# Layer 0's feed-forward: three pairs by token halves and eight by seven products in two groups, with six products ahead of the second projection

## The chip, the core and the metric

The kernel runs on one core of one Trainium2 chip. The metric is device time in microseconds (us) of one execution; the comparison is between medians of several executions. The engines are TensorE (PE; its weight loads are PEld), VectorE (DVE), ScalarE (ACT), GpSimd (POOL) and SyncE (SP), which issues most transfers. Every engine works through its own queue in order.

## What is computed

A decoder trunk of two layers on 512 tokens of width 1024, in float32. Cut to what matters here:

```python
def swiglu_ffn(x, w_up, w_down):
    gate, up = jnp.split(x @ w_up, 2, axis=-1)
    return (jax.nn.silu(gate) * up) @ w_down

# layer 0
h = h + conformer_conv(rmsnorm(h, norm_mix[0]), ...)   # pw1, GLU, causal conv of 31 taps, LayerNorm, silu, pw2
h = h + swiglu_ffn(rmsnorm(h, norm_ffn[0]), ffn_w_up[0], ffn_w_down[0])
# then K and V from rmsnorm(h), layer 1: attention and another swiglu_ffn, last rmsnorm
```

The hidden width is 2816. The change lies in layer 0, from the second projection (`pw2`) of the convolution module to the end of the feed-forward.

## The kernel before, in words

**Precision.** Float32 operands are split in a high and a low part (`whi`, `wlo` of a weight chunk; likewise of the activations), and `mm3` (L376) issues three matmuls: high by high, high by low, low by high. For every weight chunk of 512 KB ScalarE makes `whi` (L294) and VectorE `wlo` (L297). The first twelve chunks of the plan (`NATIVE`) aren't split; one plain float32 matmul stands for three.

**The plan of weights.** `chunk_plan` (L90) lists all chunks in the order of use. `advance` (L299) is called at each use: it loads up to nine chunks ahead (six `raw` buffers), splits up to three ahead, and advances `prepare` (L277) by `share` steps.

**Pairs.** The hidden width is cut into eleven pairs of 256 gate and 256 up columns. Layer 0 treats them in two ways (`HALVES0`, L35):

- Pairs 0 to 3 *by token halves*: `ffn_part` (L585) does up products, gates and down products for the first 256 tokens, later again for the last 256. A pair has four up chunks and two down chunks in each half. The second half uses the twin form `mm2` (L407): one matmul of `whi` with high and low part side by side (512 columns) and one of `wlo` (256).
- Pairs 4 to 10 *by seven products*: a Strassen scheme over the two token halves and the two halves of the 1024 inputs. `SevenPair.take` (L821) multiplies a block of weights (A11, A12, A22, or one of the sums S1 to S4) with a block of rows (B11, B12, B21, B22, or one of the sums T1 to T4), 24 matmuls of 256 columns each, and adds the results in PSUM and in a tile `c`. `gates` makes the hidden values, and one down projection over all 512 tokens follows.

The sums S of the weights are made in DRAM: SP copies a block (`copy_sums`, L268), and an accumulating transfer from the GpSimd queue adds the other block (`prepare`, L289). The copies for the first nine units (a unit is one pair of layer 0 or one part of layer 1's weights) are made in two early sets, seven and two. `share` is 0.45 steps per chunk in the halves and 1/4 in the products.

**Order.** The second token half of the convolution (`h1`) runs in the background while TensorE does the first half's `pw2`, up and down: VectorE and the pair ScalarE and GpSimd share the taps (L1010, L1002, L1003). Then come its LayerNorm: `squares`, `sums` (L1059), `scales_a` (L1068 to L1075), `scales_b`, `spread` (L1090), and eight `rows` of z (L1102 to L1104, split at L544 and L545). `job` and `pace` (L327, L337) set this by a list of points (count of chunks used, steps done). TensorE's next work after the first half is three products for first-half tokens, A12 by B21 of pairs 4, 5 and 6 (`FIRST`), whose results are kept in one `quad` buffer; and then `pw2` of the second half, which reads z.

The RMS factors of the feed-forward come from `step1` (L503 to L515: sums over channels on TensorE, `ms` on VectorE, `rs` on GpSimd, a diagonal on ScalarE) and `spread` (L529). In the first half `step1` stands between pair 0 and pair 1, and the spread after half of pair 1, when pair 0 is evacuated (L659, L662, L545).

During the second half, `Rows0.sums` makes T1 to T4 (L1296 on VectorE, then a split each), again by `job`. Then all seven pairs' products run, 46 chunks, followed by the down projection of all seven (14 chunks) and the additions to `h` (L1357), which start the next normalisation.

The program's instructions are put in each engine's queue by a scheduler that goes by a modelled time; `issue_after(x)` keeps an instruction behind `x` on the same engine.

## Time and profile before

| what | value |
|---|---|
| median of three runs | 1046.09 us (1045.9 to 1046.29) |
| the profiled execution | 1048.36 us |
| its span, first to last instruction | 1046.6 us |
| mean granted TensorE clock | 0.997 |
| bytes moved by DMA | 248.33 MB, mean 237 GB/s |
| transfers of sums: accumulates, copies one by one | 88, 52 |

Rows of the timeline read: start, length, engine, line, operation, out<-in, size, count, and in brackets the idle time before and what ended it. Rows of groups read: line, engine, operation, shape, count, then busy time and the mean of one in ns, then idle time before and its causes. Rows of stretches read: from:to, length, busy time of PE, PEld, DVE, ACT and POOL with counts, granted clock, mean share of the 16 DMA engines, GB/s. Lengths of matmuls are modelled and overlap; their pace is in the distance between starts.

The stages around the change in the profiled execution: `pw2` of the first half from 129 us, the first half's up and down from 158 us, the three products from 239 us, `pw2` of the second half from 248 us, the second half's up and down from 271 us, the products of seven from 339 us, their down projection to about 548 us.

### The profile page before, as it was taken

The numbers are of one execution on the slowest core, as the hardware profiler recorded it, in microseconds if no ns is written. First come the engines' busy times: TensorE is split into PE (matmuls) and PEld (weight loads), VectorE is DVE, ScalarE is ACT, GpSimd is POOL, SyncE is SP. The second block draws the span as 40 slices with busy tenths as digits, with TensorE's granted clock in tenths as the row PEclk, the third lists the DMA queues.
The fourth block names the chain that finished last, engine by engine and source line by source line (L and its number), as shares of the span: only waits on it lengthen the run. The fifth ranks groups of instructions, "written<-read, shape, count | busy, mean of one in ns | idle before, by whom it ended". The sixth has DMA issues, their size and how long they took to land.

```text
span 1046.6 us, 17683 instructions
## 1 busy us (share of the span) xinstructions
PE 1032.7 (99%) x6574; PEld 932.7 (89%) x6574; DVE 779.1 (74%) x1206; ACT 612.7 (59%) x1060; POOL 466.6 (45%) x563
## 2 busy tenths in 40 slices
PE   9999998999999999999999999999999999999996
PEld 8888887999988999998888877788989999898995
DVE  3999989978889786773536556678686877868677
ACT  3887896946776565552334555466655555554653
POOL 3999998940444332222214255405442334334131
PEclk9999999999999999999999999999999999999998
DMA  9999846989899988898968776845879888867742
GB/s 351 335 332 195 203 130 173 282 245 272 243 256 253 302 221 283 255 296 251 284 222 240 208 192 183 211 167 150 251 234 312 284 264 266 244 232 222 226 142 80
DMA packets 67282, 248.33 MB, mean 237 GB/s; under 512 B 7579, under 2 KB 13884, under 8 KB 66364
## 3 DMA queue, kind: packets, MB, share of 16 engines
q1 hardware_dynamic: 53804, 199.96, 54.7%
q0 software_dynamic: 12672, 46.14, 24.6%
q8 instruction: 51, 0.84, 0.3%
q10 hardware_dynamic: 720, 1.10, 0.3%
q14 instruction: 35, 0.29, 0.1%
HBM read 241.93 MB, written 97.52 MB: 324 GB/s over the span
## 4 chain that ended last, share of the span: by engine, by line
PE 91%; DVE 4%; ACT 2%; issue 1%; DMA 1%; POOL 1%; SPq 0%; DVEq 0%; ACTq 0%
PE bank L380 20%; PE bank L382 20%; PE bank L381 20%; PE bank L903 9%; PE bank L961 8%; PE bank L412 4%; PE bank L413 2%; PE bank L1442 1%; PE bank L1484 1%; PE bank L1471 1%; DVE bank L1010 1%; ACT pr L1002 1%; PE bank L1059 1%; DVE wlo L297 1%; DMA both<-in_lead_dram 1%
## 5 line engine op out<-in xcount | busy, mean ns | idle before, releaser
L297 DVE TENSOR_TENSOR wlo<-raw,whi 128x1024 fp32r<-128x1024 f32 x246 | 327.1, 1337 | 137.7 <-ACT whi L294 126.9
L294 ACT CAST whi<-raw 128x1024 fp32r<-128x1024 f32 x246 | 257.2, 1049 | 280.9 <-PE bank L381 194.9
L380 PE MATMUL bank<-quad,whi 128*128 128x256 f32 (+1 forms) x976 | 307.2, 317 | 0.0
L381 PE MATMUL bank<-quad,whi 128*128 128x256 f32 (+1 forms) x976 | 306.6, 315 | 0.0
L382 PE MATMUL bank<-quad,wlo 128*128 128x256 f32 (+1 forms) x976 | 305.7, 315 | 0.0
L380 PEld LDWEIGHTS bank<-quad,whi 128*128 128x128 f32 x976 | 185.5, 191 | 12.8 <-issue 1.6
L381 PEld LDWEIGHTS bank<-quad,whi 128*128 128x128 f32 x976 | 186.0, 191 | 11.8 <-issue 0.5
L382 PEld LDWEIGHTS bank<-quad,wlo 128*128 128x128 f32 x976 | 185.6, 191 | 11.8 <-issue 0.4
L854 POOL TENSOR_TENSOR up<-up 128x512 f32<-128x512 f32 x34 | 62.9, 1851 | 283.6 <-ACT up L851 283.6
L1003 POOL TENSOR_TENSOR pr<-pr,pr 128x256 f32<-128x256 f32 x208 | 157.5, 837 | 4.5 <-ACT pr L1002 4.2
L380 PE MATMUL bank<-rows,whi 128*128 128x256 f32 x488 | 138.0, 283 | 0.0
L381 PE MATMUL bank<-rows,whi 128*128 128x256 f32 x488 | 137.8, 282 | 0.0
L382 PE MATMUL bank<-rows,wlo 128*128 128x256 f32 x488 | 137.8, 282 | 0.0
L1010 DVE SCALAR_TENSOR_TENSOR bank<-apad,wdw,bank 128x256 f32<-128x256 f32 x248 | 112.4, 484 | 3.4
L1002 ACT ACTIVATE pr<-apad,wdw 128x256 f32<-128x256 f32 x208 | 98.5, 502 | 15.1 <-POOL pr L1003 13.2
L961 PE MATMUL bank<-quad,w 128*128 128x256 f32 x448 | 98.7, 380 | 0.0
L961 PEld LDWEIGHTS bank<-quad,w 128*128 128x128 f32 x448 | 84.9, 190 | 11.8 <-DVE bank L1010 0.2
L380 PEld LDWEIGHTS bank<-rows,whi 128*128 128x128 f32 x488 | 93.1, 191 | 0.3
L381 PEld LDWEIGHTS bank<-rows,whi 128*128 128x128 f32 x488 | 93.1, 191 | 0.3
L382 PEld LDWEIGHTS bank<-rows,wlo 128*128 128x128 f32 x488 | 93.0, 191 | 0.0
L491 POOL TENSOR_TENSOR tmp<-tmp,tmp 128x256 f32<-128x256 f32 (+1 forms) x28 | 26.8, 956 | 101.9 <-ACT tmp L487 96.7
L412 PE MATMUL bank<-quad,whi 128*128 128x512 f32 x168 | 59.7, 398 | 0.0
(229 smaller groups left out, 1632.9 us busy)
## 6 DMA issues: line engine op xcount, KB each, us to landing
raw<-in_W_dram SPq DMA_DIRECT2D x170, 512.0 KB, 5.7
raw<-sum SPq DMA_DIRECT2D x88, 512.0 KB, 5.5
sum<-in_W_dram SPq DMA_DIRECT2D x52, 512.0 KB, 6.3
sum<-in_W_dram POOLq DMA_DIRECT2D x44, 512.0 KB, 9.5
sum<-sum POOLq DMA_DIRECT2D x44, 512.0 KB, 8.8
sum<-in_W_dram SPq DMA_DIRECT2D x4, 3584.0 KB, 29.7
w<-in_W_dram SPq DMA_DIRECT2D x14, 512.0 KB, 9.7
sum<-in_W_dram SPq DMA_DIRECT2D x4, 1024.0 KB, 29.6
```

Source lines behind the costliest of these rows:

```text
L294: on_act = nc.scalar.copy(hi, src).ins
L297: latest[:] = [on_act, lo_engine[0].tensor_sub(lo, src, f32(hi)).ins]
L380: nc.tensor.matmul(out, w[0], x[0], start=start, stop=False, **kw)
L381: nc.tensor.matmul(out, w[0], x[1], start=False, stop=False, **kw)
L382: nc.tensor.matmul(out, w[1], x[0], start=False, stop=stop, **kw)
L412: nc.tensor.matmul(first[2], first[0], first[1], start=start, stop=False)
L854: pool_op(nc.gpsimd.tensor_mul(gate, gate, c[:, m, :, 1, :]))
L903: nc.tensor.matmul(out, x, w[:, ws], start=first and e == 0 and i == 0, stop=e == 1 and i == 2, skip_group_check=True)
L961: mm = nc.tensor.matmul(self.pb[:, w * W2:(w + 1) * W2], w1_of(ct, w, k), x[k] if x else xg[k][:, tok], start=k == 0, stop=k == KT - 1)
L1002: on_act = nc.scalar.mul(pr, a[:, j:j + W2], tap(j))
L1003: on_pool = pool_op(nc.gpsimd.tensor_add(pr, acc, pr))
L1010: on_dve = nc.vector.scalar_tensor_tensor(yt if i == nd - 1 else c, src, tap(i), c if i else self.shift, op0=ALU.mult, op1=ALU.add)
```

## The change

- Pairs 0 to 2 go by token halves, pairs 3 to 10 by seven products. The eight are cut in two groups of four; each group has its products and then its own down projection with its own additions to `h`. Only the last group starts the next normalisation.
- Six products (A12 of pairs 3 to 8) stand ahead of the second half's `pw2`. Their results lie in one `quad` buffer and two smaller ones in a pool `keep`. `pace` is called before each product and between its halves.
- In the first half, `step1` moves behind the first chunk of pair 1, and pair 0's evacuation behind the third.
- `stamp` holds the last matmul of `mm3`; the small matmuls of `h1`'s LayerNorm in the background are kept behind it.
- The points of `job` change for `h1` and for the sums T; `pace` is called in the loop of products, and the flush of T's job comes after the first group's products.
- `share` is 0.5 in the halves and 0.45 in the products and the first group's down projection, 0.6 in the last one's as before.
- The tiles `c` lie in `quads` for odd pairs and in `z0` for even ones; `z0` has four buffers instead of five. The early copies are now eight units and one.

```diff
-HALVES0 = ((0, 4), (4, 11))
-FIRST = (4, 5, 6)
+HALVES0 = ((0, 3), (3, 11))
+GROUPS0 = ((3, 7), (7, 11))
+FIRST = tuple(range(3, 9))
...
-    plan.extend(("up0", *step) for step in part2_products())
-    downs(*HALVES0[1])
+    for group in GROUPS0:
+        plan.extend(("up0", *step) for step in part2_products(group))
+        downs(*group)
...
+    stamp = [None]
+
     def mm3(out, w, x, start, stop, **kw):
...
-        nc.tensor.matmul(out, w[1], x[0], start=False, stop=stop, **kw)
+        stamp[0] = nc.tensor.matmul(out, w[1], x[0], start=False, stop=stop, **kw).ins
...
-                    if half == 0 and which == 1:
-                        if w == 512 or twin:
-                            rms.step1()
+                    if twin and half == 0 and which == 1 or pending and half + which == 0:
+                        rms.step1()
+                    if half == 1 and which == 0:
                         for p in pending:
                             evac(*p)
                         pending = []
-            if w == 256 and pair == lo and not twin:
-                rms.step1()
+            if pair == lo and not twin:
                 pending.append((pair, full))
...
-    def product(key, block, r, opens, closes=True):
+    def product(key, block, r, opens, between=None):
...
         for which in range(2):
+            if which and between is not None:
+                between()
...
                 for n, (_, f) in enumerate(due):
-                    f()
+                    with tc.issue_after(stamp[0]):
+                        f()
...
-                self.scales_a()
+                with tc.issue_after(stamp[0]):
+                    self.scales_a()
...
-                self.spread()
+                with tc.issue_after(stamp[0]):
+                    self.spread()
...
-        job(second, (base, 0), (base + 8, 19), (base + 13, 22), (base + 26, 40), (base + 30, 45), (base + 34, 50), (base + 35, h1.n_steps - early - 3))
+        job(second, (base, 0), (base + 8, 19), (base + 13, 22), (base + 24, 39), (base + 28, 43), (base + 29, 44), (base + 30, 44),
+            (base + 31, 46), (base + 33, 48), (base + 34, 49), (base + 37, h1.n_steps - early))
...
-        preparing[0], share[0] = prepare(), 0.45
+        preparing[0], share[0] = prepare(), 0.5
...
-    job(rows0.sums(), (base + 11, 0), (base + 19, 8), (base + 26, 14), (base + 32, 17))
+    job(rows0.sums(), (base + 10, 0), (base + 16, 8), (base + 24, 13), (base + 28, 17))
     pw2(h1.z, n1)
     ffn_part(0, 0, x0["ffn0"], HALF[1], n1.rms, twin=True)
-    flush()
...
-    share[0] = 1 / 4
...
+    share[0] = 0.45
+    for group in GROUPS0:
+        lo0, hi0 = group
+        last = hi0 == HALVES0[1][1]
...
+        for pair, a in part2_products(group):
+            if pair not in open_pairs:
+                if pair % 2:
+                    c = quads.tile([P, 2, 2, 2, 256], F32, tag="quad", name=uid("up"))
+                else:
+                    c = z0.tile([P, 2, 2, 2, 256], F32, tag="z0", name=uid("up"), bufs=4)
+                open_pairs[pair] = SevenPair("up0", pair, rows0, c, first.get(pair))
+            pace()
+            open_pairs[pair].take(a)
...
+        flush()
...
             for m in range(4):
                 nc.vector.tensor_add(h[g * 4 + m], banks[m], h[g * 4 + m])
-                nxt.on_h(g * 4 + m)
+                if last:
+                    nxt.on_h(g * 4 + m)
```

71 lines of the change are left out of this document (35 added, 36 removed).

## The prediction

> **What bounds the kernel now.** I read the first part of the page first, then TensorE's waits, then the places where they lie, then the engines by stage.
>
> ```profile
> PE 1032.7 (99%) x6574; PEld 932.7 (89%) x6574; DVE 779.1 (74%) x1206; ACT 612.7 (59%) x1060; POOL 466.6 (45%) x563
> ```
>
> Next the list of TensorE's waits over the whole run (waited for: us in total, times, longest).
>
> ```profile
> PE bank L529 <- ACT tmp L515: 2.1, 1, 2.1
> PE bank L465 <- POOL ones_m L462: 1.0, 1, 1.0
> PE bank L503 <- DVE tmp L491: 1.0, 1, 1.0
> PE bank L949 <- DVE quad L923: 0.5, 2, 0.3
> ```
>
> The reader is to see that TensorE is the bound from end to end: four kinds of wait, 4.6 us of 1046.6. Two of them, 3.18 us together, belong to the first half's RMS statistics (`step1` and the spread). Everything else is decided by how many matmuls are issued and at what pace. The pace is in the starts of neighbouring matmuls, in the timeline of TensorE: 256 columns, then the twin form (512 and 256 columns), then 512 columns in the down projection.
>
> ```profile
> 190.00 0.28 PE L380 MATMUL bank<-quad,whi 128*128 128x256 f32 x1
> 190.12 0.28 PE L381 MATMUL bank<-quad,whi 128*128 128x256 f32 x1
> ...
> 290.12 0.40 PE L412 MATMUL bank<-quad,whi 128*128 128x512 f32 x1
> 290.35 0.28 PE L413 MATMUL bank<-quad,wlo 128*128 128x256 f32 x1
> 290.47 0.39 PE L412 MATMUL bank<-quad,whi 128*128 128x512 f32 x1
> ...
> 500.00 0.39 PE L381 MATMUL bank<-quad,whi 128*128 128x512 f32 x1
> 500.22 0.39 PE L382 MATMUL bank<-quad,wlo 128*128 128x512 f32 x1
> 500.45 0.39 PE L380 MATMUL bank<-quad,whi 128*128 128x512 f32 x1
> ```
>
> So 0.12 us, 0.35 us for a twin pair, and 0.225 us. The busy column (0.28, 0.39) is a modelled length of overlapping instructions and isn't used.
>
> Close behind TensorE comes VectorE, in two stretches (length, PE, PEld, DVE, ACT, POOL busy, clock, DMA share, GB/s).
>
> ```profile
> 145.00:188.00 43.00, 39.83 (x225) 35.89 (x224) 39.88 (x64) 32.72 (x74) 37.85 (x45) 1.00 0.63 187
> 188.00:216.00 28.00, 28.00 (x232) 27.89 (x232) 27.89 (x42) 22.96 (x40) 25.13 (x27) 1.00 0.95 267
> 216.00:240.00 24.00, 24.00 (x191) 23.31 (x191) 15.64 (x25) 10.80 (x15) 8.08 (x9) 1.00 0.88 230
> 302.00:346.00 44.00, 44.00 (x270) 39.15 (x269) 42.64 (x52) 27.47 (x40) 20.05 (x19) 1.00 0.95 262
> ```
>
> VectorE is full while the second half's convolution is finished (to 219 us) and again while the sums T1 to T4 are made (302 to 346 us). Both lie in the stages that the change shortens.
>
> **The change part by part.** (1) *Matmuls.* Pair 3 by halves costs 96 + 48 matmuls of 256 columns in the first half, 144 x 0.12 = 17.3 us, and 32 + 16 twin pairs in the second, 48 x 0.35 = 16.8 us: 34.1 us. By seven products it costs 7 x 24 x 0.12 = 20.2 us, and its down projection 48 x 0.225 = 10.8 us: 31.0 us. Term: **-3.1 us**. Six products ahead instead of three is the same work in another place; splitting in two groups adds none on TensorE.
>
> (2) *`step1` a chunk later.* Now it stands before pair 1 and TensorE waits for the last square sum; the next rows are that wait, the spread's, and what VectorE did between.
>
> ```profile
> 174.05 0.61 PE L503 MATMUL bank<-ones_c,tmp 128*128 128x1 f32 x4 [1.05 <-DVE tmp L491]
> 182.63 0.70 PE L529 MATMUL bank<-tmp,ones_m 128*128 128x256 f32 x2 [2.13 <-ACT tmp L515]
> ...
> 173.92 5.12 DVE L297 TENSOR_TENSOR wlo<-raw,whi 128x1024 fp32r<-128x1024 f32 x3
> 178.96 2.05 DVE L1010 SCALAR_TENSOR_TENSOR bank<-apad,wdw,bank 128x256 f32<-128x256 f32 x4
> 180.92 0.15 DVE L505 TENSOR_SCALAR ms<-bank 128x2 f32<-128x2 f32 x1
> ```
>
> One chunk of 24 matmuls (2.9 us) ahead of `step1` covers its 1.05 us. The spread keeps its distance, two chunks; its lateness comes from the `ms` instruction standing 7 us behind three splits and four taps. In the new order it is reached by TensorE at about 182, a little before 182.6; if a fourth split gets ahead of `ms`, it is 2.8 us late instead. Bounds of the two together: -3.2 to -0.4; I take **-1.7** (the first wait gone, a third of the second).
>
> (3) *The convolution's deadline.* TensorE reaches `pw2(h1)` earlier: 72 matmuls fewer (8.6 us) and what (2) gives. VectorE loses six splits, adds three, and loses one evacuation (L659 and two like it, 2 us). The rows below carry the evacuation's group and the chain's end: last tap, sums, scales, spread, first rows of z.
>
> ```profile
> L659 DVE TENSOR_TENSOR tmp<-bank,rsbc 128x512 f32<-128x512 f32 x4 | 2.6, 679 | 0.0
> ...
> 218.64 0.86 DVE L1010 SCALAR_TENSOR_TENSOR y<-apad,wdw,bank 128x256 f32<-128x256 f32 x2
> ...
> 219.25 2.42 POOL L1014 TENSOR_TENSOR y<-y,pr 128x256 f32<-128x256 f32 x2 [5.31 <-DVE y L1010]
> ...
> 224.34 0.59 PE L1059 MATMUL bank<-y,ones_m 128*128 128x256 f32 x2
> ...
> 229.18 0.95 PE L1068 MATMUL bank<-ident,tmp 128*128 128x1 f32 x8
> ...
> 238.46 1.02 PE L1090 MATMUL bank<-tmp,ones_m 128*128 128x512 f32 x2
> ...
> 245.18 0.75 DVE L545 TENSOR_TENSOR quad<-tmp,quad 128x256 fp32r<-128x256 f32 x2
> ```
>
> From the last tap to z's first two rows it takes 26 us, of which some 8 are waiting for places in TensorE's order. Counting 14 chunks, six products and 4 us of small matmuls from 173.0 us (174.05 less its wait), the new `pw2(h1)` is reached at about 235, so the last tap has to end near 215; VectorE's queue, two splits and an evacuation shorter up to there but with the half's `h` updates in it, ends it between 212 and 217. Six products give 17 us for sums, scales, spread and rows, where 28 us lay between last tap and `pw2(h1)` (238.46, the spread's 0.5 and three products make 247.6). What is queued behind: the first `pw2` chunk waits for z's rows, and all TensorE work behind it. Bounds 0 to +4; I take **+1.0**.
>
> (4) *The second half.* 16.8 us of TensorE go, but only six splits of 1.34 us and an evacuation (four L645 and a split) from VectorE, 10.3 us. From the start of T1 to the products there are 9.5 chunks instead of 12: VectorE brings 2 us more backlog into the products, where it is 73% busy and catches up. `flush` is gone, so T4's split may end inside the first products; T4 is the seventh needed. Bounds 0 to +2.5; I take **+0.5**.
>
> ```profile
> L297 DVE TENSOR_TENSOR wlo<-raw,whi 128x1024 fp32r<-128x1024 f32 x246 | 327.1, 1337 | 137.7 <-ACT whi L294 126.9 <-DMA bias<-fd 4.2 <-DMA raw<-in_W_dram 4.2
> ...
> L645 DVE TENSOR_TENSOR tmp<-bank,tmp 128x256 f32<-128x256 f32 x16 | 6.2, 414 | 1.0 <-ACT tmp L644 0.8
> ...
> L1357 DVE TENSOR_TENSOR h<-bank,h 128x512 f32<-128x512 f32 x8 | 5.5, 686 | 0.1
> ...
> 344.00:472.00 128.00, 128.00 (x1060) 127.33 (x1060) 93.74 (x106) 71.63 (x94) 34.82 (x25) 1.00 0.91 273
> ```
>
> (5) *The sums' transfers.* Pair 3 needs four sums more. `share` 0.45 in the products instead of 0.25 makes 25 x 0.45 = 11 accumulates in each group of 25 products, with a copy to go with most of them in the second group.
>
> ```profile
> q1 hardware_dynamic: 53804, 199.96, 54.7%
> q0 software_dynamic: 12672, 46.14, 24.6%
> ...
> raw<-in_W_dram SPq DMA_DIRECT2D x170, 512.0 KB, 5.7
> ...
> sum<-in_W_dram POOLq DMA_DIRECT2D x44, 512.0 KB, 9.5
> ...
> 350.00:360.00 10.00, 10.00 (x86) 10.00 (x85) 7.73 (x10) 4.30 (x5) 2.14 (x1) 1.00 1.03 333
> ...
> SPq L261 <- DVE wlo L297: 653.0, 221, 13.1
> ```
>
> By the queues' rows a load or copy of 0.524 MB takes the 16 engines 1.50 us (54.7% of 1046.6 for 199.96 MB) and an accumulate 2.93 us (24.6%, 88 of them). A product of 2.88 us then asks for 1.50 + 0.45 x (2.93 + 1.50) = 3.5 us in the second group, 346 GB/s, and some 3.2 in the first: more than the engines have. Cover: loads wait for a free buffer (the 653 us), six buffers of 2.88 us less the landing of 5.7 leave 11 us, and the eight down chunks between the groups (5.4 us each) let the queue catch up. The second group's excess, at the share of 1.03 seen, is 0.5 us x 25 = 12 us, just the cover. Bounds 0 to +6; I take **+0.4**. None of (3) to (5) can gain: TensorE doesn't wait there now.
>
> (6) *At nothing.* Eight more `h` additions on VectorE (0.69 us each) lie beside the second group. The down projection of group 1 needs the last pair's gates only after three chunks (16 us). Buffers: four of `z0`, with odd pairs in `quads`, replace five; at most ten or eleven of eleven `quads` are held. The early copies cover nine units as before, in another division. Were one of these covers gone, it costs an evacuation of one to two microseconds.
>
> Sum: -3.1 - 1.7 + 1.0 + 0.5 + 0.4 = **-2.9 us**. The profiled execution took 1048.36 us (span 1046.6 and 1.8 around it), which makes 1045.5; the median shown is 1046.09, 2.3 lower, and I put the change on that: **1043.2 us**.
>
> **The rivals.** *Everything hides*: the spread's wait goes too and (3) to (5) cost nothing, -3.1 - 3.2 = -6.3, 1039.8. For it: after 10 us TensorE waits nowhere else now. Against: VectorE is full in both stretches.
>
> *VectorE is the clock of the first half*: the last tap ends at 217 or later, z comes 3 to 4 us late, the spread still waits, T's backlog costs 1 or 2. -3.1 - 0.4 + 3.5 + 0.5 = +0.5 at its middle, between -1.5 and +2: 1046.6. The change then shortens the matmuls but not the time. For it: 27.89 of 28 us busy. Against: 216 to 240 has 8 us to spare, and the chain's places were loose.
>
> *The weight loads run dry in the products* (the slower side). [...] If a load lands twice as late as 5.7 us, half of the cover is left; then the first group waits little and the second 6 us: -2.9 - 0.4 + 6.4 = +3.1, 1049.2. It decides from the point where a product's transfers exceed 2.88 us by more than cover over 25, that is 0.25 us with 6 us of cover. For it: 3.5 us asked. Against: the row at 350 moved 333 GB/s with TensorE never waiting. [...]
>
> **How the numbers follow.** Forecast 0.42, everything hides 0.13, VectorE 0.26, loads run dry 0.19. The likeliest gives 1043.2, its own range 1041.5 to 1044.0. From the bounds, 1040.0 to 1049.0 leaves out about 0.1 on each side. About 0.2% (2.1 us) is what a measurement of this kernel can tell from no change: faster 0.55 (the first two), same 0.25, slower 0.20 (the last, and the tail of VectorE's).
>
> **What would show it.** Right: matmul counts of the twin form down by 96, of 512 columns up by 48, the same pace, L503 without a wait, L529's under 2 us; no wait of TensorE before `pw2(h1)` above 1 us, and none on weights in the products. Wrong: a wait on the z rows or on L1059 of several microseconds (3); waits on `wlo` at the first products (4); ACT's cast waiting for `raw` DMAs, landings past 11 us and TensorE waiting on `whi` in the second group (5).

## The result, and the profile after

The changed kernel takes 1055.22 us (median of six, 1053.6 to 1057.82), the kernel before 1045.99 us (six, 1045.65 to 1046.54): ratio 1.0088, 95% interval 1.0077 to 1.0099. It is slower by 9.2 us where 2.9 us less was forecast, and beyond the upper end of the range. The profiled execution took 1054.15 us (span 1052.4 us, mean granted clock 0.996).

Line numbers have moved: the split is now L299 (L297 before), its cast on ScalarE L296 (L294), GpSimd's addition of a tap L1010 (L1003), VectorE's tap L1017 (L1010), `mm3` L384 to L386, the spread of the norm's scale L533, the addition of the block made early to the first product L836 (L831).

First the list of TensorE's waits in the changed kernel (waited for: us in total, times, longest).

```profile
PE bank L386 <- DVE wlo L299: 3.5, 2, 3.0
PE bank L384 <- DVE up L836: 1.7, 1, 1.7
PE bank L533 <- ACT tmp L519: 1.5, 1, 1.5
PE bank L385 <- DVE quad L549: 1.3, 2, 1.1
PE bank L384 <- ACT whi L296: 1.1, 1, 1.1
PE bank L469 <- POOL ones_m L466: 1.1, 1, 1.1
PE bank L956 <- DVE quad L928: 0.2, 1, 0.2
```

Of before's four kinds one is gone (L507, the former L503, no longer waits) and two are smaller (the spread waits 1.5 instead of 2.1 us, L956, the former L949, 0.2 instead of 0.5), but four kinds are new: L386, L385 and two at L384. In time the larger waits lie in two places. The rows of TensorE's timeline, each with the idle time before it and what ended it:

```profile
182.88 0.70 PE L533 MATMUL bank<-tmp,ones_m 128*128 128x256 f32 x2 [1.49 <-ACT tmp L519]
...
196.17 0.39 PE L386 MATMUL bank<-quad,wlo 128*128 128x256 f32 x1 [0.51 <-DVE wlo L299]
...
200.32 0.38 PE L385 MATMUL bank<-quad,whi 128*128 128x256 f32 x1 [1.13 <-DVE quad L549]
...
206.61 0.39 PE L386 MATMUL bank<-quad,wlo 128*128 128x256 f32 x1 [3.04 <-DVE wlo L299]
...
326.05 0.39 PE L384 MATMUL bank<-quad,whi 128*128 128x256 f32 x1 [1.06 <-ACT whi L296]
...
328.27 0.39 PE L384 MATMUL bank<-rows,whi 128*128 128x256 f32 x1 [1.72 <-DVE up L836]
```

6.2 us stand in the first half's up projection, some 40 to 60 us ahead of `pw2(h1)`; 2.8 us at the start of the products. At `pw2(h1)` itself TensorE waits 0.2 us, and none of the listed waits ends with a weight transfer.

What VectorE and GpSimd did during the longest wait, in their timelines (start, length, engine, line, operation):

```profile
199.20 0.48 DVE L1017 SCALAR_TENSOR_TENSOR bank<-apad,wdw,bank 128x256 f32<-128x256 f32 x1
...
200.79 0.47 DVE L1017 SCALAR_TENSOR_TENSOR bank<-apad,wdw,bank 128x256 f32<-128x256 f32 x1
201.18 5.38 DVE L299 TENSOR_TENSOR wlo<-raw,whi 128x1024 fp32r<-128x1024 f32 x1
...
207.47 1.21 DVE L299 TENSOR_TENSOR wlo<-raw,whi 128x1024 fp32r<-128x1024 f32 x1
```

```profile
198.15 2.40 POOL L1010 TENSOR_TENSOR pr<-pr,pr 128x256 f32<-128x256 f32 x2
200.49 0.80 POOL L291 DMA_DIRECT2D sum<-in_W_dram  x1
201.06 4.40 POOL L1010 TENSOR_TENSOR pr<-pr,pr 128x256 f32<-128x256 f32 x6
205.19 1.04 POOL L291 DMA_DIRECT2D sum<-sum  x1
```

A split of the same form takes 1.21 us at 207.47 and 5.38 us at 201.18. GpSimd began six additions 0.12 us before the long one, and they ended at 205.46; 1.21 us before the split's end is 205.35. So the split seems to have done its work after the whole row, and VectorE stood for it. It was not waiting for its cast on ScalarE: the last cast ahead of it ended at 201.46. The taps on VectorE, which have one operand in PSUM (`bank`), take as long when GpSimd adds beside them (0.48 us at 199.20; from 60 to 262 us a mean of 0.485 over 165) as when it is idle (0.482 over 15).

The kernel before has a row of six additions at nearly the same place, and there a split gets in. Its rows of VectorE and GpSimd:

```profile
202.88 1.78 DVE L297 TENSOR_TENSOR wlo<-raw,whi 128x1024 fp32r<-128x1024 f32 x1
```

```profile
200.88 5.78 POOL L1003 TENSOR_TENSOR pr<-pr,pr 128x256 f32<-128x256 f32 x6
```

The split comes in after one addition, and the addition behind it (at 203.54 us in the trace) takes 1.72 us instead of 0.73: here the loss is shared, 0.57 us on the split and 0.99 us on the addition. So the number of additions in a row does not decide alone. What also differs in the traces is how far the records of neighbouring additions overlap: in the long row of the changed kernel each begins about 0.3 us before the one ahead of it ends, in before's row 0.04 us. Over the 18 traces that have these additions (60 to 262 us), 35 splits met two GpSimd instructions (issues of transfers not counted) that overlap by 0.2 us or more, and 33 of them took over 2 us; 97 met instructions that overlap by at most 0.1 us, and 3 did. No run sets this overlap by itself, so it is a sign and not a shown cause.

Two stretches, by engines (length, busy time of PE, PEld, DVE, ACT and POOL with counts, clock, DMA share, GB/s), the first of them shown for before too:

```profile
188.00:216.00 28.00, 23.23 (x172) 22.32 (x171) 27.93 (x33) 17.70 (x31) 21.01 (x25) 0.94 0.89 220
...
208.00:212.00 4.00, 4.00 (x22) 3.90 (x22) 4.00 (x7) 3.85 (x8) 2.68 (x3) 0.65 0.97 249
```

In 188 to 216 us VectorE looks as full as before (27.93 us against 27.89), but with 33 instructions instead of 42: what fills it is standing. And behind the 3.04 us wait the granted clock is down (0.65 over 208 to 212; in the clock's records it is half for 3.41 us, from 207.4). The starts of matmuls show it too:

```profile
207.07 0.28 PE L386 MATMUL bank<-quad,wlo 128*128 128x256 f32 x1
207.19 0.28 PE L384 MATMUL bank<-quad,whi 128*128 128x256 f32 x1
...
207.68 0.42 PE L384 MATMUL bank<-quad,whi 128*128 128x256 f32 x1
207.89 0.42 PE L385 MATMUL bank<-quad,whi 128*128 128x256 f32 x1
```

0.12 us apart at first, 0.21 after. So a wait of 3.0 us cost about 4.5 to 4.7, as an estimate: by the starts, 16 matmuls at 0.21 instead of 0.12 us, 1.5 us come on top, by the granted clock half of the 3.41 us.

### The profile page after: what moved, and what is told of

The parts are those of the page before. It is cut to its first block, busy times and chain, and to the rows that moved or that the text cites. A ratio compares the mean times of both kernels' runs of the same rounds, so it can differ in the third digit from the quotient of the medians.

```text
span 1052.4 us, 17644 instructions
## 1 busy us (share of the span) xinstructions
PE 1032.3 (98%) x6550; PEld 931.5 (89%) x6550; DVE 789.3 (75%) x1212; ACT 610.2 (58%) x1057; POOL 471.3 (45%) x567
## 4 chain that ended last, share of the span: by engine, by line
PE 67%; DVE 1%; ACT 0%; POOL 0%; issue 0%
PE bank L384 18%; PE bank L386 18%; PE bank L385 18%; PE bank L908 9%; PE bank L1462 1%; PE bank L1504 1%; PE bank L1491 1%; PE bank L1620 0%; DVE room L1622 0%; PE bank L1583 0%; DVE room L1631 0%; PE bank L533 0%; PE bank L507 0%; ACT room L1637 0%; POOL rs L1630 0%; DVE room L1635 0%
## 5 line engine op out<-in xcount | busy, mean ns | idle before, releaser
L299 DVE TENSOR_TENSOR wlo<-raw,whi 128x1024 fp32r<-128x1024 f32 x243 | 327.4, 1355 | 126.9 <-ACT whi L296 126.5
L296 ACT CAST whi<-raw 128x1024 fp32r<-128x1024 f32 x243 | 253.8, 1048 | 279.9 <-PE bank L385 197.2
L386 PE MATMUL bank<-quad,wlo 128*128 128x256 f32 (+1 forms) x976 | 307.5, 318 | 3.6 <-DVE wlo L299 3.5
L385 PE MATMUL bank<-quad,whi 128*128 128x256 f32 (+1 forms) x976 | 309.0, 318 | 1.3 <-DVE quad L549 1.3
L384 PE MATMUL bank<-quad,whi 128*128 128x256 f32 (+1 forms) x976 | 308.5, 320 | 1.1 <-ACT whi L296 1.1
L859 POOL TENSOR_TENSOR up<-up 128x512 f32<-128x512 f32 x36 | 67.5, 1875 | 327.3 <-ACT up L856 327.3
L386 PEld LDWEIGHTS bank<-quad,wlo 128*128 128x128 f32 x976 | 186.0, 191 | 16.7 <-DVE wlo L299 4.2
L385 PEld LDWEIGHTS bank<-quad,whi 128*128 128x128 f32 x976 | 186.4, 191 | 14.3 <-DVE quad L549 1.9
L384 PEld LDWEIGHTS bank<-quad,whi 128*128 128x128 f32 x976 | 185.8, 191 | 14.8 <-issue 1.3
L1010 POOL TENSOR_TENSOR pr<-pr,pr 128x256 f32<-128x256 f32 x208 | 153.6, 790 | 6.8 <-ACT pr L1009 6.7
L384 PE MATMUL bank<-rows,whi 128*128 128x256 f32 x512 | 144.9, 283 | 1.7 <-DVE up L836 1.7
L385 PE MATMUL bank<-rows,whi 128*128 128x256 f32 x512 | 144.6, 282 | 0.0
L386 PE MATMUL bank<-rows,wlo 128*128 128x256 f32 x512 | 144.6, 282 | 0.0
L1017 DVE SCALAR_TENSOR_TENSOR bank<-apad,wdw,bank 128x256 f32<-128x256 f32 x248 | 112.5, 485 | 3.5
L384 PEld LDWEIGHTS bank<-rows,whi 128*128 128x128 f32 x512 | 97.6, 191 | 2.2 <-DVE up L836 1.9
L385 PEld LDWEIGHTS bank<-rows,whi 128*128 128x128 f32 x512 | 97.6, 191 | 0.3
L386 PEld LDWEIGHTS bank<-rows,wlo 128*128 128x128 f32 x512 | 97.6, 191 | 0.0
L908 PE MATMUL bank<-wlo,fhi 128*128 128x512 f32 x140 | 55.2, 394 | 0.0
```

The costliest lines, as they stand in the source:

```text
L296: on_act = nc.scalar.copy(hi, src).ins
L299: latest[:] = [on_act, lo_engine[0].tensor_sub(lo, src, f32(hi)).ins]
L384: nc.tensor.matmul(out, w[0], x[0], start=start, stop=False, **kw)
L385: nc.tensor.matmul(out, w[0], x[1], start=False, stop=False, **kw)
L386: stamp[0] = nc.tensor.matmul(out, w[1], x[0], start=False, stop=stop, **kw).ins
L859: pool_op(nc.gpsimd.tensor_mul(gate, gate, c[:, m, :, 1, :]))
```

## The experiments

"The kernel before" below is the one measured with each run on the same chip; ratios are to it, with 95% intervals. These medians of before agree within 0.6 us, so two runs are compared by their medians. The theories: **L**, VectorE's splits (two operands in SBUF) are shut out while GpSimd's additions run back to back; **V**, VectorE simply has too much to do in the first half; **Q**, the waits at the products' start come from VectorE's queue order there.

### The additions taken away

`no_adds` is the changed kernel, `no_adds_before` the kernel before, with the second half's tap additions on GpSimd left out (its taps on ScalarE are made but not summed):

```diff
-    on_pool = pool_op(nc.gpsimd.tensor_add(pr, acc, pr))
+    on_pool = on_act if self.hf else pool_op(nc.gpsimd.tensor_add(pr, acc, pr))
```

> The changed kernel without GpSimd's additions of the second half's taps (the 104 adds of h1 between tap products are left out, so its convolution is only partly summed; VectorE's own taps, splits and all matmuls stay). Theory L (GpSimd's runs of adds shut VectorE's two-input subtractions out: a split of 1.21 us took 4.6 and 5.4 us): splits of the first half back at 1.2 to 1.3 us, no wait of TensorE on wlo between 190 and 210 us, no half clock there; 9 us less there, 1055.2 becomes about 1046. Rival V (VectorE has simply too much work before the earlier deadline): its instructions are the same in number, so the waits stay and the time stays within 2 us of 1055.

> The kernel before with the same adds of h1 left out. L: its splits get shorter too (mean of 1.45 us in 145 to 219 us goes to about 1.25), the waits at step1 and the spread shrink from 3.2 to 1 to 2 us: 1044 to 1045.5. V: the same, 1046. Beside the run no_adds it shows what the other parts of the change cost or bring where the adds don't disturb: by the matmul term alone no_adds should be 3.1 us below this one, by the waits at the first products seen in the changed kernel about equal.

`no_adds`: 1048.19 us, ratio 1.0023 (1.0012 to 1.0034), 7.0 us less than the changed kernel. `no_adds_before`: 1046.30, ratio 1.0004 (0.9994 to 1.0013). Leaving the additions out gives nothing in the kernel before and seven microseconds in the changed one, though VectorE does the same work. Put the other way, the change costs 9.2 us with the additions and 1.9 us without them. In `no_adds_before` the waits at `step1` and the spread are gone, too, but the time is not the 1044 to 1045.5 us that L expected from that. The group of splits between 172 and 212 us (count, then busy us and mean ns of one), in before, after and `no_adds`:

```profile
L297 DVE TENSOR_TENSOR wlo<-raw,whi 128x1024 fp32r<-128x1024 f32 x14 | 20.8, 1495 | 2.5 <-ACT whi L294 2.5
```

```profile
L299 DVE TENSOR_TENSOR wlo<-raw,whi 128x1024 fp32r<-128x1024 f32 x10 | 26.5, 2660 | 0.3 <-ACT whi L296 0.3
```

```profile
L299 DVE TENSOR_TENSOR wlo<-raw,whi 128x1024 fp32r<-128x1024 f32 x12 | 14.6, 1220 | 1.9 <-ACT whi L296 1.7
```

The mean goes from 1495 to 2660 ns, and to 1220 without additions. The waits of the first half's up projection are gone in `no_adds` (0.2 us is left at `pw2(h1)`, and 1.4 us at the first `pw2`, ahead of the stages compared here, which `no_adds_before` has too). Those at the products' start stay, number for number, here with 3.41 us of half clock behind them (from 321.8 us in the clock's records):

```profile
319.07 0.39 PE L384 MATMUL bank<-quad,whi 128*128 128x256 f32 x1 [1.06 <-ACT whi L296]
...
321.30 0.39 PE L384 MATMUL bank<-rows,whi 128*128 128x256 f32 x1 [1.72 <-DVE up L836]
```

This speaks for L and against V, and shows that there are two separate places.

### The place of step1

`step_back` is the changed kernel with `step1` and the evacuation of pair 0 where they stood before; `step_only` is the kernel before with them in the new place (the same edit the other way round).

```diff
-                    if twin and half == 0 and which == 1 or pending and half + which == 0:
-                        rms.step1()
-                    if half == 1 and which == 0:
+                    if half == 0 and which == 1:
+                        if w == 512 or twin:
+                            rms.step1()
                         for p in pending:
                             evac(*p)
...
-            if pair == lo and not twin:
+            if w == 256 and pair == lo and not twin:
+                rms.step1()
                 pending.append((pair, full))
```

> The changed kernel with step1 and pair 0's evacuation at their old places. If the new places made the trouble (taps queued on ScalarE ahead of the diagonal, so that GpSimd's adds lie ready in a heap): waits on wlo in 190 to 210 us gone, the old 1.0 and 2.1 us waits back, about 1049. If the earlier deadline and the missing pair made it (V), the waits on wlo stay and the time stays at 1053 to 1056.

> The kernel before with step1 and the evacuation at the new places alone. If the new places made the trouble: splits of 3 us and more appear in 180 to 210 us, waits on wlo, 1047 to 1051. If not: the wait at step1 goes, 1044.5 to 1046.

`step_back`: 1058.12 us, ratio 1.0114 (1.0098 to 1.0131), 2.9 us more than the changed kernel, and outside both expectations: no wait on `wlo` is left, but the long splits are there (5.49, 4.37 and 5.57 us), and TensorE meets them elsewhere, with 3.33 us at the spread and 2.64 us on a split of hidden values (L548). `step_only`: 1045.78, ratio 1.0002 (0.9993 to 1.0012). So the move alone costs nothing. In `step_only`'s profile both waits of `step1` and spread are gone, splits of 3.44 and 4.35 us and one wait of 1.0 us on a split are new, and the time is that of before; so the 3.2 us that the profiled execution of before showed were not to be had from its median.

### Only the grouping

`groups_only` has four pairs by halves, three products ahead, old `step1` and due points, but the seven pairs in groups of four and three with their own down projections, no `flush`, `share` 0.45.

```diff
-HALVES0 = ((0, 3), (3, 11))
-GROUPS0 = ((3, 7), (7, 11))
-FIRST = tuple(range(3, 9))
+HALVES0 = ((0, 4), (4, 11))
+GROUPS0 = ((4, 8), (8, 11))
+FIRST = (4, 5, 6)
```

> The kernel before with four pairs by halves again and three products ahead, its step1 and its due points, but with the changed kernel's grouping: groups of four and three at the products, so that the matmul work per product is the one of before. If the grouping costs nothing, the time is that of the kernel before, 1045 to 1046.5 us, and the loss of the changed kernel lies in the first half and at the product start; if the grouping has a price of its own (T later, other order of the second half's sums), it is above 1047.

1045.93 us, ratio 1.0005 (0.9995 to 1.0014): the grouping, its second set of additions to `h` and the higher `share` are free. Its profiled execution has a span of 1043.8 us and one wait of 1.0 us in the whole of layer 0, so it serves as a clean ledger (starts of stages in us, from the trace; the expected column is the prediction's 0.12 us a matmul):

| stage | groups_only | changed | difference | expected |
|---|---|---|---|---|
| `pw2` of the first half to the twin stage | 128.95 to 268.27 | 128.57 to 267.69 | -0.2 | -17.3 + 8.6 = -8.7 |
| twin stage | to 336.68 | to 319.11 | -17.0 | -16.8 |
| products and down projections | to 555.55 | to 563.67 | +25.7 | 31.0 - 8.6 = +22.4 |
| rest | to 1043.82 | to 1052.37 | +0.4 | 0 |

The matmuling is as worked out. The first half loses 8.5 us (waits and the half clock behind them), the products 3.3.

### Shorter rows of additions in the changed kernel

Three ways: `pr3` with three buffers of `pr`, `points_late` with two due points later, `pool_less` with two taps fewer on GpSimd in each channel tile of the second half, and the due points stretched to match (not in the diff).

```diff
-pr = cv.tile([P, W2], F32, tag="pr", name=uid("pr"), bufs=8)
+pr = cv.tile([P, W2], F32, tag="pr", name=uid("pr"), bufs=3)
```

```diff
-(base + 24, 39), (base + 28, 43), (base + 29, 44)
+(base + 26, 39), (base + 28, 42), (base + 29, 44)
```

```diff
-N_POOL = ((13, 13, 12, 12), (17, 15, 15, 15))
+N_POOL = ((13, 13, 12, 12), (15, 13, 13, 13))
```

> The changed kernel with three buffers instead of eight for GpSimd's products `pr`, so that GpSimd can never hold more than three tap additions ready to run one behind the other (the changed kernel shows rows of six of them, 4.40 and 5.14 us long, over splits of 5.38 and 4.55 us). Theory L (a split with two SBUF inputs does not get in while GpSimd's additions run back to back): the splits of the first half fall from a mean of 2.66 us to under 2 us, TensorE's waits of the first half from 6.6 us in all to under 2 us, the time to 1049 to 1052 us. Rival V (VectorE simply has too much to do in the first half): the work is the same, so the waits stay within 1 us and the time at 1054 to 1057, or a little more where the taps now wait for a buffer.

> The changed kernel with four of the due points of the first half's convolution one or two units later, so that the same taps are spread over more of the matmuls. Theory L: shorter rows of GpSimd's additions, so TensorE's waits of the first half fall from 6.6 us to about 3, and the time to 1051 to 1054 us; if the rows of additions only move, no change (1054 to 1057). Rival V (VectorE's total): the same work at other times gives a gain only if there is room later, at most 1 us.

> The changed kernel with two taps fewer on GpSimd in each channel tile of the second half's convolution (15, 13, 13 and 13 instead of 17, 15, 15 and 15), which go to VectorE: 16 additions on GpSimd less, 16 taps of VectorE more. The due points are stretched in proportion. Theory L: GpSimd's additions are what holds the splits up, so the splits of the first half get shorter (mean under 2.2 us against 2.66) and TensorE's waits of the first half fall to 2 to 5 us: 1050 to 1054 us. Rival V: VectorE is what has too much to do, so 16 more taps make it worse, waits of 8 us and more: above 1056 us.

All three missed the time that L gave. `pr3`: 1176.0 us, ratio 1.1242 (1.1215 to 1.1269). No split is stretched any more, which is L's half of the expectation, but each addition now waits for ScalarE's next product, 1.34 us a tap, and TensorE waits for the convolution:

```profile
188.98 0.72 POOL L1010 TENSOR_TENSOR pr<-pr,pr 128x256 f32<-128x256 f32 x1 [0.62 <-ACT pr L1009]
```

```profile
PE bank L1066 <- POOL y L1021: 72.3, 3, 34.4
```

`points_late`: 1057.4, ratio 1.0113 (1.0095 to 1.0131); its profile is of its slowest execution, 1060.39 us. The wait on `wlo` falls from 3.5 to 0.8 us, but the convolution is late by 2.1 us and 10.24 us of half clock follow:

```profile
PE bank L1066 <- POOL y L1021: 2.5, 2, 2.1
...
PE bank L386 <- DVE wlo L299: 0.8, 1, 0.8
```

```profile
229.00:238.00 9.00, 8.06 (x32) 7.17 (x33) 0.65 (x4) 2.39 (x6) 3.46 (x7) 0.50 0.37 91
```

`pool_less`: 1064.9, ratio 1.0184 (1.0169 to 1.0199). L was right about the splits (mean 1730 ns instead of 2660, wait on `wlo` 0.5 us) and V about the time: the taps handed to VectorE end later, GpSimd idles for them, and TensorE waits for both.

```profile
PE bank L1066 <- POOL y L1021: 6.8, 1, 6.8
PE bank L533 <- ACT tmp L519: 3.7, 1, 3.7
```

```profile
234.84 1.41 POOL L1021 TENSOR_TENSOR y<-y,pr 128x256 f32<-128x256 f32 x2 [17.31 <-DVE y L1017]
```

So L names the mechanism, but in these three the first half has no slack on either engine: what is taken from GpSimd's rows comes back at the convolution's deadline. That deadline is term (3) of the prediction, met from the other side.

### The start of the products

`t_early` moves the sums T three units forward; `copy_first` takes VectorE's addition at L836 off TensorE's path.

```diff
-job(rows0.sums(), (base + 10, 0), (base + 16, 8), (base + 24, 13), (base + 28, 17))
+job(rows0.sums(), (base + 10, 0), (base + 13, 8), (base + 21, 14), (base + 25, 17))
```

```diff
-nc.vector.tensor_add(c11, r, self.early)
+nc.scalar.copy(c11, r)
+pool_op(nc.gpsimd.tensor_add(c11, c11, self.early))
```

> The changed kernel with the due points of the sums T of layer 0's raw columns three units earlier, so that the last split of T and its h updates no longer stand in VectorE's queue ahead of the first product's addition at line 836. Theory Q (the waits of 1.06 and 1.72 us at the start of the products come from VectorE's order there): both waits together under 1 us, no stretch of half clock behind them, 2 to 4 us less: 1051 to 1053 us. Rival: the sums land on VectorE in the first half, where it is starved already, and the waits there grow by as much: 1054 to 1058.

> The changed kernel, where the first product of a pair of the second half goes from its bank by a copy on ScalarE, and the block made in the first half is added to it afterwards by GpSimd, in place of VectorE's addition at line 836. Theory Q2 (VectorE is behind at the end of the shortened twin stage, whatever stands in its queue, and TensorE waits for it through the bank of line 836): the wait of 1.72 us there goes, and the one of 1.06 us on ScalarE stays or grows by at most 0.7 us; 1 to 3 us less than the changed kernel's 1055: 1052 to 1054 us. Rival: TensorE then waits for the next split of weights from the same late VectorE, with the same 2.8 us in all: 1054 to 1057.

`t_early`: 1057.13 us, ratio 1.0109 (1.0094 to 1.0124). Theory Q, as it was put, falls: T's split is gone from the place, but the additions to `h` stand there instead, L836 comes at 328.67 and the wait is 2.28 us; 1.7 us more are lost near the end of the twin stage. VectorE's queue at the place in the changed kernel and in `t_early`:

```profile
323.67 1.68 DVE L299 TENSOR_TENSOR wlo<-raw,whi 128x1024 fp32r<-128x1024 f32 x1
325.27 2.34 DVE L549 TENSOR_TENSOR quad<-plain,quad 128x512 fp32r<-128x512 f32 x2
327.54 0.68 DVE L836 TENSOR_TENSOR up<-bank,quad 128x512 f32<-128x512 f32 x1
```

```profile
324.19 2.75 DVE L611 TENSOR_TENSOR h<-h,tmp 128x256 f32<-128x256 f32 x2
326.87 1.21 DVE L299 TENSOR_TENSOR wlo<-raw,whi 128x1024 fp32r<-128x1024 f32 x1
328.01 0.74 DVE L609 TENSOR_TENSOR tmp<-bank,tmp 128x256 f32<-128x256 f32 x2
328.67 0.68 DVE L836 TENSOR_TENSOR up<-bank,quad 128x512 f32<-128x512 f32 x1
```

`copy_first`: 1051.97, ratio 1.0060 (1.0045 to 1.0075), 3.2 us less than the changed kernel, and both waits at the place are gone. This speaks for Q2: VectorE is behind at the end of a twin stage that is 17 us shorter, in whatever order, and TensorE meets it at the bank of L836. Q2 left the 1.06 us wait on ScalarE's cast standing; why it went too is not shown.

### More cover, and both repairs

`all_first` has all eight first products ahead of `pw2(h1)`, with the due points spread over them; `all_copy` has that and `copy_first`'s edit.

```diff
-FIRST = tuple(range(3, 9))
+FIRST = tuple(range(3, 11))
...
-(base + 24, 39), (base + 28, 43), (base + 29, 44), (base + 30, 44),
-(base + 31, 46), (base + 33, 48), (base + 34, 49), (base + 37, h1.n_steps - early)
+(base + 26, 40), (base + 32, 43), (base + 33, 44), (base + 34, 44),
+(base + 35, 46), (base + 37, 48), (base + 38, 49), (base + 41, h1.n_steps - early)
```

> The changed kernel with all eight first products ahead of the second projection instead of six (two more products, 5.7 us more of TensorE ahead of the deadline of the first half's convolution, and 5.7 us less in the second half), and the due points of the convolution spread over that. The matmul work is the same as in the changed kernel. Theory L (GpSimd's rows of tap additions shut VectorE's two-input splits out, and TensorE's cover there is too short): with more cover the additions are spread, the waits of the first half fall from 6.6 us to under 2 and the half clock behind them goes, the waits of 2.8 us at the start of the products stay: 1047 to 1050 us. Rival: a late split stops TensorE as soon as one row of additions stands on it, however long the cover, and the waits stay at 5 us or more: 1053 to 1057.

> Both edits together: all eight first products ahead of the second projection, and ScalarE and GpSimd in place of VectorE's addition at line 836. If both causes are what the two theories say, their gains add: no wait of TensorE of over 1 us between 150 us and 340 us, and 1043 to 1047 us, at or below the kernel before; if either theory fails, 1050 or more.

`all_first`: 1052.98 us, ratio 1.0075 (1.0058 to 1.0091), 2.2 us less than the changed kernel where 5 to 8 were expected: one row of six additions still stands on a split, with a wait of 2.21 us behind it. This is nearer to the rival. `all_copy`: 1047.95, ratio 1.0021 (1.0012 to 1.0031), 7.3 us less: 1.9 us more than the sum of the two gains (2.2 + 3.2), and still 2.3 us above before, between the two outcomes expected. The long split of `all_copy` and the row on it:

```profile
198.20 5.73 DVE L299 TENSOR_TENSOR wlo<-raw,whi 128x1024 fp32r<-128x1024 f32 x1
```

```profile
198.42 4.42 POOL L1011 TENSOR_TENSOR pr<-pr,pr 128x256 f32<-128x256 f32 x6
```

### How long a row is

Four variants of `all_copy`: `ac_pr6` and `ac_pr5` have six and five buffers of `pr` (first diff), `ac_late` has two steps of the convolution later (second diff), `ac_pr6_late` both edits.

```diff
-pr = cv.tile([P, W2], F32, tag="pr", name=uid("pr"), bufs=8)
+pr = cv.tile([P, W2], F32, tag="pr", name=uid("pr"), bufs=6)
```

```diff
-(base, 0), (base + 8, 19), (base + 13, 22), (base + 26, 40)
+(base, 0), (base + 8, 19), (base + 13, 22), (base + 26, 38)
```

> The kernel with both repairs (all eight first products ahead, ScalarE and GpSimd in place of VectorE's addition at line 836), with six buffers of `pr` instead of eight. Theory B (a row of additions is as long as the buffers of `pr` less the two accumulators, and a split waits out the row): rows of at most four, the long split of 5.73 us falls to 4.0 to 4.6 us, TensorE's wait of 2.2 us on it to 0.5 to 1.0, and the time from 1047.95 to 1045.5 to 1047 us. Rival D (the row is as long as the work that the due points have let loose; buffers only hold it back): the split stays over 5 us, or the convolution comes late by the buffers and the time rises above 1048.5.

> As the one before, with five buffers of `pr`. Theory B: rows of at most three, the long split at 3.3 to 3.9 us, no wait of TensorE on it, 1044.5 to 1046.5 us, unless the convolution, which has only three products in hand, comes late; then waits on GpSimd's y at the sums and above 1050. Rival D: as with six buffers, worse.

> The kernel with both repairs and eight buffers of `pr`, with two steps fewer of the convolution due in the first half's matmul stage (38 instead of 40 at unit 26) and two more in the first products behind it. Rival D: fewer steps let loose there, so shorter rows, the wait of 2.2 us at most 1 and the time 1045 to 1047. Theory B: rows of six come all the same, only elsewhere: one split of over 5 us stays, and the time within 1 us of 1047.95, unless the convolution comes late.

> Both: six buffers and two steps later. If both theories hold a part, 1044 to 1046 us, below the kernel before's 1045.7 or at it; if the convolution comes late, waits on GpSimd's y and above 1048.

`ac_pr6`: 1046.57 us, ratio 1.0008 (0.9999 to 1.0016). The longest split is 4.17 us over a row of four, and no wait on `wlo` is left:

```profile
205.94 4.17 DVE L299 TENSOR_TENSOR wlo<-raw,whi 128x1024 fp32r<-128x1024 f32 x1
```

```profile
205.74 3.06 POOL L1011 TENSOR_TENSOR pr<-pr,pr 128x256 f32<-128x256 f32 x4
```

`ac_pr5`: 1056.28, ratio 1.0101 (1.0087 to 1.0115): splits of 4.85, 5.01 and 8.22 us, so the count of buffers alone does not set a row (theory B falls as a rule), and the waits are back. `ac_late`: 1046.13, ratio 1.0003 (0.9994 to 1.0012): the longest split between 178 and 260 us is 4.07 us and the time is in the range of rival D; one split of 5.50 us at 171 us, ahead of the steps moved, stays. `ac_pr6_late`: 1047.84, ratio 1.0022 (1.0013 to 1.0031): the two together are worse than each, and neither expectation for both held. A likely reading, not shown by a run of its own, is that rows follow how many products are ready when GpSimd turns to them, and that buffers and due points are two of several things that decide it.

### The last wait

`ac_pr6`'s profile has one larger wait, 2.38 us at the spread: `rs` on GpSimd (L511) stands behind a row of GpSimd's own work, additions and squares. `ac_pr6_evac` and `ac_late_evac` put only the evacuation, and with it the spread, one chunk later.

```diff
-                    if half == 1 and which == 0:
+                    if half == 1 and which == 1:
                         for p in pending:
```

> The kernel with both repairs and six buffers of `pr`, in which the first pair's evacuation, and with it the spread of the norm's scale over the partitions, comes one chunk of weights (2.85 us of matmuls) later. If the wait of 2.38 us at the spread (the scale `rs` behind GpSimd's additions) is what is left of the loss, it goes, and the time falls from 1046.57 to 1043.5 to 1045 us, below the kernel before's 1045.8. Rival: the banks of the first pair come free too late for the third, TensorE waits there for as long, and the time stays at 1046 to 1047.

> The same one edit on the kernel with both repairs, eight buffers and two steps of the convolution later, which has a wait of 1.39 us at the spread and 1.3 us behind it: 1044 to 1045.5 us if the spread's wait is what counts, 1046 if the banks or the splits take its place.

`ac_pr6_evac`: 1046.84 us, ratio 1.0012 (1.0003 to 1.0021). The wait at the spread falls to 0.62 us, and a split makes TensorE wait instead (the rival's time, but not by its banks):

```profile
185.81 0.70 PE L533 MATMUL bank<-tmp,ones_m 128*128 128x256 f32 x2 [0.62 <-ACT tmp L519]
...
191.54 0.39 PE L386 MATMUL bank<-quad,wlo 128*128 128x256 f32 x1 [1.74 <-DVE wlo L299]
```

`ac_late_evac`: 1053.11, ratio 1.0067 (1.0055 to 1.0080): a split of 5.97 us under another row, a wait of 4.39 us, two stretches of half clock, and outside both expectations. With a shift of one chunk other splits meet other rows.

No version beat the kernel before. The best, `ac_late` and `ac_pr6`, can't be told from it.

## Why the prediction was wrong

**(1) Matmuls, -3.1.** Right: the twin form has 288 matmuls instead of 384, its stage gave -17.0 for -16.8, and the products' +25.7 is the +22.4 worked out with 2.8 us of waits; the -8.7 of the first half is covered up by its waits.

**(2) `step1` a chunk later, -1.7.** The mechanism was right (L507 no longer waits, the spread waits 1.49 us instead of 2.13), the term was not: the waits were those of one execution 2.3 us above the median, and the gain was put on the median. `step_only` measures 0 (ratio 1.0002). Why the spread was late was only half seen, too: `rs` on GpSimd, 0.71 us in before, takes 1.63 us beside a split in the changed kernel, and in `ac_pr6` it stands in a row as the splits do.

**(3) The convolution's deadline, +1.0, bounds 0 to +4.** This is the step that failed. It looked for the price at z's rows, ahead of `pw2(h1)`, and worked VectorE's progress out from counts of instructions at their usual length ("VectorE's queue, two splits and an evacuation shorter up to there"); for a wait on `wlo` in the first half's own up projection it had no term. By its count the last tap ends between 212 and 217 us. Without the additions it does (217.1 us in `no_adds`); in the changed kernel it ends at 225.6 us, for splits of 1.2 us took 3.3 to 5.5 us beside GpSimd's additions. TensorE ran out of `wlo` in the middle of the up projection and reached `pw2(h1)` at 244.5 us instead of 235, so that only 0.2 us of waiting was left at the place where the price was looked for. Measured: 7.0 us by `no_adds`, 8.5 us by the ledger of stages with the half clock, where the upper bound was 4.

Which part of the change brings the rows onto the splits was not isolated. The convolution is let loose faster (39 steps by unit 24 instead of 40 by unit 26), but `all_copy`, with before's points up to unit 26, still has a split of 5.73 us. The move of `step1` alone brings long splits (`step_only`), and without the move they come as well (`step_back`). A row of before that could have warned was in view: splits of 5.12 us for three, that is 1.7 us each, beside GpSimd's taps.

**(4) The second half, +0.5, bounds 0 to +2.5.** Right place and engine (VectorE's backlog carried into the products), wrong size and wrong victim: TensorE waits not for T4 or `wlo`, but for the addition at L836 behind T4's split, and the bank it holds. 3.2 us by `copy_first`.

**(5) The sums' transfers, +0.4, and the slower rival.** No profile's list of TensorE's waits has one on a transfer; `groups_only`, with the higher `share` and the accumulates of seven pairs, is at 1.0005. The rival that weight loads run dry, on which the slower side of the range stood, did not occur. It supposed loads that land after twice 5.7 us, which the changed kernel's trace does not show as the usual case: in its products and down projections (319 to 564 us) the 60 weight loads landed after 7.4 us at the median and 13.5 at most, the 32 accumulates after 11.3 us at the median, and neither TensorE nor ScalarE's cast has a wait that ended with a load. **(6) At nothing:** right, by the same run.

**The rivals.** *Everything hides* is out by the waits. Nearest was *VectorE is the clock of the first half*, +0.5 us in the text: the right stage and engine, but as a full queue whose excess is a few splits. As such it fell too: in `no_adds` VectorE has the same work, and the first half's up projection no wait. No rival reached the measured time; the slowest stood at 1049.2 us. The sum of what was measured apart: -2.8 (stages' matmuls), 0, +7.0, +3.2, 0, together +7.4 of 9.2 us; the rest is not assigned.

**The clock.** The prediction had no term for what follows a wait. In the traces' clock records half clock within the run (the first and last microseconds left aside) lasts 3.41 us in the changed kernel and in `no_adds`, and 10.24 us, three times as long, in `points_late`. It does not follow from a wait's length alone: the 1.06 and 1.72 us at the products' start bring none in the changed kernel's profile and 3.41 us in `no_adds`'s; 2.28 us at the products' start was followed by it in `t_early`, 2.38 us at the spread in `ac_pr6` was not. The two stretches behind the last two, in that order (the clock is the third number from the end):

```profile
330.00:333.00 3.00, 3.00 (x16) 3.00 (x15) 3.00 (x5) 0.00 (x0) 2.73 (x4) 0.50 1.12 246
```

```profile
184.00:188.00 4.00, 4.00 (x35) 3.97 (x35) 3.81 (x6) 4.00 (x10) 4.00 (x6) 1.00 0.98 179
```

Waits of 2.12 us (`points_late`) and 2.28 us (`t_early`) were enough for it, then; what decides which wait is followed by it, no run shows.

**What stays open.** Whether the 3.1 us can be had: each repair moved a wait in the first half, and the best medians are still 3 to 4 us above what the matmuls alone would give. `ac_pr6`'s profile is of its fastest execution (1044.54 us; median 1046.57), so its waits are not those of its typical run. And why some rows let a split in and others shut it out: the overlap of their records goes with it, but no run sets that, and none changed the split's operands.

## What to carry to other kernels

A busy column of an engine says how long its instructions lasted, not how much they did: compare the mean length of one form between stages before taking 27.9 of 28 us as work. Where VectorE's two-operand work feeds TensorE while GpSimd works in the background, price the background by the longest row that a split may have to wait out (5.38 us over six additions in the changed kernel), not by its sum. Before's rows were as long and let the splits in, so this is a bound that need not be reached; and whether cover for TensorE is enough was not shown, since two more products ahead left a wait of 2.21 us (`all_first`). And a gain read off waits of a single execution counts against that execution only; put against a median, it needs a sign that the median has these waits.

## What the runs showed of the hardware

A subtraction on VectorE with both operands in SBUF waited out a whole row of GpSimd's additions in the changed kernel and its variants: 5.38 us over six, 5.73 over six (`all_copy`), 4.17 over four (`ac_pr6`), 1.21 alone. In such a row GpSimd lost nothing (six in 4.40 us, against 0.72 to 0.73 for one). In the kernel before, within a row of six, both lost: 1.78 us for the subtraction and 1.72 us for the addition behind it. VectorE's taps with one operand in PSUM kept their 0.47 to 0.49 us.

When a long split came in can be estimated from its end less the 1.21 us that it takes alone. In the changed kernel that is 205.35 us for the split of 5.38 us, 191.27 for one of 4.55 and 185.89 for one of 3.30, and in these three GpSimd was issuing a transfer (L291, from 205.19, 191.13 and 185.47 us); in a fourth, of 5.51 us from 171.18, it was at an addition (of squares, L1052). What lets a split in after one addition (0.73 us) in one row and only after the row in another was not shown. The order of the starts does not tell the long rows apart: in the changed kernel the row's record begins 0.12 us before the long split's, in `all_copy` 0.22 us after it.

A short wait of TensorE cost more than itself in some executions and not in others: half clock lasted 3.41 us (1.5 to 1.7 us of work, by the estimate above) behind a wait of 3.04 us in the changed kernel and behind 1.06 and 1.72 us close together in `no_adds`, at least 3 us (330 to 333 us) behind 2.28 us in `t_early`, and 10.24 us behind 2.12 us in `points_late`. The range of the changed kernel's times (1053.6 to 1057.82 us, against 1045.65 to 1046.54 before) fits that; it was not shown apart.
